# Modulation weights in ten tiles, paired low parts, scaling on GpSimd, half of group 0's rows on ScalarE

## The chip, the core and the metric

The kernel runs on one core of one Trainium2 chip. A core has five engines that take instructions each from a queue of its own: TensorE (PE, matrix products; its weight loads are shown apart as PEld), VectorE (DVE), ScalarE (ACT), GpSimd (POOL) and SyncE (SP), which here only issues DMA transfers. Engines wait for each other by semaphores; within one queue, order is kept. The metric is the device time of one execution in microseconds (us). A profile records one execution; "span" is the time from its first to its last instruction.

## The reference

One layer of a hybrid backbone. 2048 latent tokens `x` and 256 context tokens `ctx`, 1024 wide:

```
shift, scale, gate     = split(silu(c)     @ w_ada + b_ada)
shift_c, scale_c, ...  = split(silu(c_ctx) @ w_ada + b_ada)
h  = rmsnorm(x,   norm_w) * (1 + scale)   + shift
hc = rmsnorm(ctx, norm_w) * (1 + scale_c) + shift_c
p  = h  @ w_in                # 9216 columns: q, i, zf, zb, gate of 8 heads; 4 of the convolution
pc = hc @ w_in[:, :5120]
```

Then a gated linear recurrence in both directions over each head (its start state comes from the context), a gated three-tap convolution for the other half of the columns, `y = concat @ w_out`, `x + gate * y`, and a final RMS norm. All in float32.

## The kernel before

**Products.** To keep float32 precision with 16-bit matmuls, each operand is split into a high part (a cast to f16) and a low part (the difference, in f16 too); a product is three matmuls. The projection `h @ w_in` is done for a group of 512 tokens (`GW`; four groups) and two column blocks at a time by Winograd's form of Strassen's scheme (`seven`): seven products of half-size operands in place of eight. The token side of a group thus has seven operands, B11, T1, T2, B21, T3, B22, T4, each for four k (128 rows of the contraction). Group 0 starts differently: its first stretch ("plain" units) uses the four unsplit quarters B11, B12, B21, B22, and its T1 to T4 are made late (`late_turn`), in the fourth stretch.

**Start.** The order in the program is: load four x tiles of group 0 (128 tokens x 1024), their squares (L220), load and split the first pair of projection weights (`next_w(0)` at L1250: z gates of head 0), then `modulate` (L177). This multiplies the two conditioning vectors by the first 2048 columns of w_ada: for each of eight k two tiles of 128 x 1024 f32 are loaded (L182), four matmuls (L184) add to the PSUM tile `pada`, and `between(k)` transposes block k of group 0's scaled tokens and copies it out raw (L232, L239, L241). After k = 3 (`VQ_AT`) the second weight pair (V and Q of head 0) is loaded and split. The tiles of w_ada live in `f_tile` and `k_tile`, two of each: two k at a time. `modulate_end` and `affine` (L189, L198) turn `pada` into a scale and a shift per row. Then `turn` makes group 0's quarters: `rows(k)` scales and shifts the eight raw blocks in place (L246), `store` casts on ScalarE (L265) or GpSimd (L263), and subtracts on VectorE (L266).

**Weights.** `load_pair` (L327) loads two column blocks of w_in into "stage" tiles (three in all), sums absolute values on ScalarE (L341), finds a power-of-two scale (a one-column matmul, L139, and three small VectorE steps, L145 to L147), and splits them (L151 high on ScalarE, L152 low on VectorE) with four additions. A stage tile comes free with the last low part that reads it.

**Groups 1 to 3 and the context.** `norm_group` gives the steps: load, squares, a reciprocal root on VectorE (L125 to L131), scaling of each token tile by it (L225, VectorE), transposes (L232), rows (`rows`, L250 on ScalarE from PSUM), `combine` (the additions between quarters, L297 to L309) and `store`. Each operand of a k is a pair (high, low) of 256 columns, in a tile of tag "u" (eight of 1 KB a partition; the evacuations of `seven` use the same tag), and goes to DRAM (L268) by a DMA of SyncE. Once a group is complete, its seven operands are loaded back for all k (L1231) into the "hop" tiles (nine).

**Order.** The work is cut into 50 stretches; a stretch has units (products) and steps (norms, scan of a head, gates, weight splits), which are laid between the matmuls by weights (`PACE`). Stretch 0 holds the plain units and the context's units, and beside them the norms of the context and of group 1; stretches 1 and 2 hold the rest of group 2 and 3; stretch 3 group 0's late turns. Each engine then takes its instructions in an order fixed at build time: by the program's order, but something that is ready may pass something that isn't. A tile's slot is given again when all its readers are done, a store's landing included. The pools that matter: "ring" (ten slots of 2 KB: rows, combine's `t`, the scan's v, q, ks, kT, A, gates of the context, gate units), "u", "hop", "Q" (six), "stage".

Of the kernel before, what the change touches and what calls it, by code (L numbers as in the profile page):

```python
# [9 lines left out]
F32 = mybir.dt.float32  # L10
F16 = mybir.dt.float16
# [8 lines left out]
P = 128  # L20
# [40 lines left out]
def hybrid_layer(ctx: ExitStack, tc, x, cx, w_ada, b_ada, w_in, w_out, fnorm_w, small_d, masks, ident_d, sel_d, out):  # L61
# [29 lines left out]
    def pa_t(nm):  # L91
        return pa.tile([P, 512], F32, tag="pa", name=nm)
# [16 lines left out]
    def flat(t):  # L109
        return t.rearrange("p a b -> p (a b)")  # L110
# [63 lines left out]
        S.activation(sg2, cc, AF.Sigmoid)  # L174
        V.tensor_tensor(sc32[:, :, 0:2], cc, sg2, ALU.mult)

    def modulate(between):  # L177
        pada = pa_t("pada")
        for k in range(KT):
            wa = [(f_tile if j == 0 else k_tile)(f"wa{k}{j}") for j in range(2)]  # L180
            for j in range(2):
                SY.dma_start(flat(wa[j]), w_ada[0, k * P:(k + 1) * P, j * D:(j + 1) * D])  # L182
            for j in range(4):
                PE.matmul(pada[32 * j:32 * j + 32, :], sc32[:, k, :], wa[j // 2][:, j % 2],  # L184
                          start=k == 0, stop=k == KT - 1)
            between(k)
        return pada

# [19 lines left out]
    def norm_group(ntile, src, row0, m, nm, first_ops=None, space=q_tile):  # L208
        n = ntile * P
        xs = []  # L210
        ssq = sp.tile([P, 16], F32, tag="ssq", name=f"ssq_{nm}", bufs=4)

        def load(i):
            xt = space(f"xt_{nm}{i}")
            xt = flat(xt) if len(xt.shape) == 3 else xt
            SY.dma_start(xt, src[0, row0 + i * P: row0 + (i + 1) * P, :])
            xs.append(xt)

        def square(i):
            S.activation(junk, xs[i], AF.Square, accum_out=ssq[:, i:i + 1])  # L220

        def norm():
            rstd = rsqrt(ssq[:, :ntile], ntile, 1.0 / D, nm)
            for i in range(ntile):
                V.tensor_scalar(xs[i], xs[i], rstd[:, i:i + 1], None, ALU.mult)  # L225

        raws = {}

        def transposed(k):
            pt = pa_t(f"xT_{nm}{k}")  # L230
            for i in range(ntile):
                PE.transpose(pt[:, i * P:(i + 1) * P], xs[i][:, k * P:(k + 1) * P], ident)  # L232
            return pt

        def raw(k):
            pt = transposed(k)
            raws[k] = ring(f"h32_{nm}{k}")
            if k % 2:
                V.tensor_copy(raws[k], pt)  # L239
            else:  # L240
                S.activation(raws[k], pt, AF.Copy)  # L241

        def rows(k):
            if k in raws:
                h32 = raws[k]
                V.tensor_scalar(h32, h32, ab[:, m, 0, k:k + 1], ab[:, m, 1, k:k + 1], ALU.mult, ALU.add)  # L246
                return h32
            pt = transposed(k)
            h32 = ring(f"h32_{nm}{k}")
            S.activation(h32[:, :n], pt[:, :n], AF.Identity, bias=ab[:, m, 1, k:k + 1], scale=ab[:, m, 0, k:k + 1])  # L250
            return h32

        def store(op, k, src, cast, low=V):
            if m:
                i = ("B1", "B2", "D").index(op)
                hi, lo = hc[:, i, 0, k], hc[:, i, 1, k]
            elif first_ops is not None and op in first_ops:
                hi, lo = first_ops[op][:, 0, k], first_ops[op][:, 1, k]
            else:
                pair = hp.tile([P, 2, HW], F16, tag="u", name=f"hp{op}_{nm}{k}", bufs=8)  # L260
                hi, lo = pair[:, 0], pair[:, 1]
            if cast is G:
                G.tensor_scalar(hi, src, 1.0, 0.0, ALU.mult, ALU.add)  # L263
            else:
                S.activation(hi, src, AF.Copy)  # L265
            low.tensor_tensor(lo, src, hi, ALU.subtract)  # L266
            if m == 0 and (first_ops is None or op not in first_ops):
                SY.dma_start(Hd[row0 // GW][op][:, :, k], pair)  # L268
# [24 lines left out]
        def combine(k, a, b, whole):  # L293
            b11, b12, b21, b22 = a[:, :HW], a[:, HW:], b[:, :HW], b[:, HW:]
            t = ring(f"ht_{nm}{k}")
            t1, t2 = t[:, :HW], t[:, HW:]
            V.tensor_tensor(t1, b12, b11, ALU.subtract)  # L297
            if whole:
                store("B11", k, b11, S)
            store("T1", k, t1, G)  # L300
            V.tensor_tensor(t2, b22, t1, ALU.subtract)
            store("T2", k, t2, S)
            if whole:
                store("B21", k, b21, G)
            V.tensor_tensor(b12, b22, b12, ALU.subtract)
            store("T3", k, b12, S)
            if whole:
                store("B22", k, b22, G)
            V.tensor_tensor(b21, b21, t2, ALU.subtract)  # L309
            store("T4", k, b21, G)  # L310

        return ([paced("load", lambda i=i: load(i)) for i in range(ntile)],
                [paced("square", lambda i=i: square(i)) for i in range(ntile)] + [paced("norm", norm)],
                [paced("turn", lambda k=k: turn(k)) for k in range(HK)],
                [paced("late", lambda k=k: late_turn(k)) for k in range(HK)],
                [paced(0.0, lambda k=k: raw(k)) for k in range(KT)])
# [915 lines left out]
            hop.setdefault(wi_, {})[o] = t  # L1232
            taken[0] += 1

    x1_tiles = [hp.tile([P, D], F32, tag="hop", name=f"x1_{i}") for i in range(NCH)]
    x1_norm = norm_group(NCH, x, GW, 0, "x1", None, lambda nm: x1_tiles.pop(0))
    plain = {o: hop_tile(f"hop0{o}") for o in ("B11", "B12", "B21", "B22")}
    a21_ = hop_tile("a21")
    extra_a21 = [[a21_[:, hl, :, i * P:(i + 1) * P] for hl in range(2)] for i in range(2)]
# [9 lines left out]
    small_params()  # L1249
    next_w(0)  # L1250

    def between(k):
        first[4][k][1]()
        if k == VQ_AT:
            next_w(0)

    pada = modulate(between)
    ctx_norm = norm_group(2, cx, 0, 1, "c")
    for _, st in ctx_norm[0] + x1_norm[0]:
        st()  # L1260
# [263 lines left out]
```

## Time and profile before

| | |
|---|---|
| time, median of 3 | 2226.86 us (2222.09 to 2229.01) |
| profiled execution | 2224.16 us, span 2222.2 us |
| busy: PE, PEld | 2113.2 us (95%), 1466.6 us (66%) |
| busy: DVE, ACT, POOL | 1659.9 us (75%), 1158.3 us (52%), 112.5 us (5%) |
| mean granted TensorE clock | 0.988 |
| DMA | 309.89 MB, mean 139 GB/s |

How to read the lines below. A group's line has line, engine, operation, out<-in by the program's names, count, busy us, mean ns, and the idle time before it with what ended that. A source's line has min/median/max ns and first and last start. In a timeline: start, length, engine, line, operation, and in brackets the idle time of the engine before it and what it waited for. The chain of waits is followed back from the last instruction; "issue" is time in which nothing shown was waited for. SPq is SyncE's queue. The line numbers are those of the kernel before.

### The profile page before, as it was taken

To read this page: it belongs to the slowest core of one execution; us is meant where nothing else is said; L and a number is where in the kernel's file an instruction comes from. 1 tells how busy PE (TensorE), PEld (TensorE's weight loads), DVE (VectorE), ACT (ScalarE), POOL (GpSimd) and SP (SyncE) were. 2 spreads that over 40 slices of the span, in tenths; PEclk is the share of its full clock that TensorE was granted. 3 is DMA by queue.
4 is the path that set the end of the run, shared out by engine and by line. 5 is a ranking of instruction groups with operands and counts; after the bars stand their busy time and mean duration, and the time that the engine had idled before them with its cause. 6 is when DMAs were issued, how large, how long until landed. Compare 5 with 4: busy or idle time off the path is not lost.

```text
span 2222.2 us, 51962 instructions
## 1 busy us (share of the span) xinstructions
PE 2113.2 (95%) x21563; PEld 1466.6 (66%) x21563; DVE 1659.9 (75%) x3515; ACT 1158.3 (52%) x2313; POOL 112.5 (5%) x207
## 2 busy tenths in 40 slices
PE   4889899999999999999999999999999999999998
PEld 1767688888888888888888887444444444444443
DVE  6987877968779778788687786587678646677775
ACT  6655655665567555666676554354445313333332
POOL 0211100000000000000000000000000000000000
PEclk8889999999999999999999999999999999999999
DMA  8664343433243333333543357842343224633321
GB/s 324 223 212 169 103 137 103 153 95 117 82 158 112 106 120 119 108 111 122 191 134 131 126 183 248 240 137 101 108 138 116 68 90 157 232 106 122 120 99 57
DMA packets 191040, 309.89 MB, mean 139 GB/s; under 512 B 13138, under 2 KB 123090, under 8 KB 189012
## 3 DMA queue, kind: packets, MB, share of 16 engines
q1 hardware_dynamic: 188644, 302.64, 41.5%
q8 instruction: 169, 2.77, 0.5%
q10 hardware_dynamic: 2160, 3.93, 0.5%
q14 instruction: 67, 0.55, 0.1%
HBM read 241.50 MB, written 65.01 MB: 138 GB/s over the span
## 4 chain that ended last, share of the span: by engine, by line
PE 66%; DVE 15%; DMA 7%; ACT 6%; issue 4%; SPq 1%; POOL 1%; POOLq 0%; DVEq 0%; ACTq 0%
PE sa L839 8%; PE sa L841 7%; PE sa L840 7%; PE sb L839 4%; PE sb L840 3%; PE sb L841 3%; DMA ws_p<-in_w_in 3%; PE sa_o L839 2%; PE sa_o L841 2%; PE sa_o L840 2%; PE A L554 2%; PE T L602 2%; PE sc L839 2%; PE sc L841 2%; PE sc L840 2%
## 5 line engine op out<-in xcount | busy, mean ns | idle before, releaser
L840 PEld LDWEIGHTS <-e_p 128*128 128x128 f16 x1368 | 134.8, 99 | 66.8 <-issue 17.1
L414 DVE TENSOR_TENSOR K<-K,tot 128x512 f32<-128x512 f32 x192 | 132.0, 688 | 61.8 <-PE A L578 24.6
L839 PEld LDWEIGHTS <-e_p 128*128 128x128 f16 x1368 | 134.5, 98 | 60.2 <-issue 3.3
L841 PEld LDWEIGHTS <-e_p 128*128 128x128 f16 x1368 | 134.8, 99 | 53.1 <-issue 0.8
L421 DVE TENSOR_TENSOR Q<-Q,tot 128x512 f32<-128x512 f32 x192 | 132.6, 691 | 33.3 <-PE A L554 32.9
L537 ACT ACTIVATE km<-K 128x512 f32<-128x512 f32 x160 | 109.1, 686 | 86.3 <-DVE K L414 60.6
L840 PEld LDWEIGHTS <-whib_p 128*128 128x128 f16 x912 | 89.2, 98 | 45.5 <-issue 13.3
L586 POOL COPY A<-Ac 32x128 f32<-32x128 f32 x128 | 66.4, 519 | 1007.1 <-ACT A L582 649.2
L839 PEld LDWEIGHTS <-whib_p 128*128 128x128 f16 x912 | 89.1, 98 | 40.8 <-issue 3.7
L840 PEld LDWEIGHTS <-whia_p 128*128 128x128 f16 x912 | 89.3, 98 | 37.9 <-issue 6.3
L839 PEld LDWEIGHTS <-whia_p 128*128 128x128 f16 x912 | 89.2, 98 | 37.5 <-issue 0.8
L841 PEld LDWEIGHTS <-wloa_p 128*128 128x128 f16 x912 | 89.3, 98 | 34.3
L841 PEld LDWEIGHTS <-wlob_p 128*128 128x128 f16 x912 | 89.2, 98 | 34.3
L151 ACT ACTIVATE e_p<-ws_p,sc_p 128x512 f16<-128x512 f32 x108 | 77.2, 716 | 61.4 <-DVE ws_p L376 39.4
L341 ACT ACTIVATE junk<-ws_p 128x1024 f16<-128x1024 f32 x72 | 76.0, 1055 | 55.7 <-DMA ws_p<-in_w_in 55.2
L846 ACT ACTIVATE u<-sa,sx_w 128x256 f32<-128x256 f32 (+1 forms) x114 | 59.8, 524 | 70.9 <-PE sa L841 56.1
L554 PE MATMUL A<-Q,km 128*32 128x32 f32 x5120 | 77.9, 202 | 12.4 <-DVE Q L421 6.4
L554 PEld LDWEIGHTS A<-Q,km 128*32 128x32 f32 x5120 | 58.9, 112 | 46.4 <-issue 20.3
L762 ACT ACTIVATE cv<-c,small 128x512 f32<-128x512 f32 (+1 forms) x36 | 24.2, 671 | 109.2 <-DVE c L780 48.9
L152 DVE SCALAR_TENSOR_TENSOR e_p<-ws_p,sc_p,e_p 128x512 f16<-128x512 f32 x108 | 78.0, 743 | 2.5 <-ACT e_p L151 2.4
L846 ACT ACTIVATE p<-sb,sx_w 128x256 f32<-128x256 f32 (+1 forms) x114 | 59.3, 520 | 35.6 <-PE sb L841 34.0
L846 ACT ACTIVATE p<-sa,sx_w 128x256 f32<-128x256 f32 (+1 forms) x114 | 58.8, 516 | 32.2 <-PE sa L841 32.1
(865 smaller groups left out, 6881.7 us busy)
## 6 DMA issues: line engine op xcount, KB each, us to landing
ws_p<-in_w_in SPq DMA_DIRECT2D x72, 512.0 KB, 4.4
y_o<-yT SPq DMA_DIRECT2D x32, 512.0 KB, 3.8
wa<-in_w_ada SPq DMA_DIRECT2D x16, 512.0 KB, 5.4
Gd<-zs SPq DMA_DIRECT2D x32, 256.0 KB, 3.5
sg<-Gd SPq DMA_DIRECT2D x32, 256.0 KB, 4.1
yT<-y SPq DMA_DIRECT2D x32, 256.0 KB, 2.3
wos_a<-in_w_out SPq DMA_DIRECT2D x16, 512.0 KB, 4.6
yT<-sg SPq DMA_DIRECT2D x64, 128.0 KB, 2.6
```

The source lines that it names most:

```text
L151: S.activation(hi, src, AF.Copy, scale=st[:, 0:1])
L152: V.scalar_tensor_tensor(lo, src, st[:, 0:1], hi, ALU.mult, ALU.subtract)
L341: S.activation(junk.rearrange("p (k n) -> p k n", k=KT), stage[i], AF.Abs, accum_out=r)
L414: V.tensor_tensor(m, m, sub(cur, nb + 1, [[2, np_], [-(nb + 1), 2], [0, B]]), ALU.mult)
L421: V.tensor_tensor(m, m, sub(cur, 1, [[2, np_], [nb - 1, 2], [0, B]]), ALU.mult)
L537: S.activation(sub(s.km, 0, [[2 * B, n // (2 * B)], [B, 2], [1, B]]), mix(s.K, n, B, n // (2 * B)), AF.Copy)
L554: PE.matmul(pt[j * SB:(j + 1) * SB, ch * SB:(ch + 1) * SB], s.km[:, o:o + SB], mix(s.qf, n, B, SB // (2 * B), o), start=True, stop=True)
L586: G.tensor_copy(A3[js, :, js], s.Ac[js])
L839: PE.matmul(ps, hi[:, k], rh, start=start and k == 0, stop=False, skip_group_check=not start)
L840: PE.matmul(ps, hi[:, k], right(name, 1, k), start=False, stop=False, skip_group_check=not start)
L841: PE.matmul(ps, lo[:, k], rh, start=False, stop=k == nk - 1, skip_group_check=not start)
L846: S.activation(r, ps, AF.Copy, scale=sx)
```

## The change

- **Ten tiles.** `modulate` loads w_ada into ten tiles: two f, two K, two Q and four hop tiles, so five k at a time. The loads of the first five k are issued ahead of all of its matmuls; a further k is loaded when the matmuls of the k five before it are in the program. The V/Q weight pair is loaded (and split) after the load of k = 3, ahead of the modulation's matmuls and of the raw transposes, where it stood after `between(3)`. The hop tiles of group 1's tokens are taken when they are loaded, behind the modulation, and no longer ahead of everything.
- **Scaling on GpSimd.** The scaling of token tiles goes to GpSimd for the context and groups 1 to 3; group 0's stays on VectorE.
- **Half of group 0's rows on ScalarE.** Of the eight raw blocks, the four with k >= HK are scaled and shifted by ScalarE.
- **Rows of two operands.** In `combine`, T1 and T2 lie side by side in one tile, B11 and T3 in another, B21 and B22 in the third. For groups 1 to 3 these are cast and subtracted 512 columns at a time (`store2`), T4 alone with 256; for group 0's late turns T1 with T2, T3 and T4 alone. The (high, low) pairs come from "ring" in place of "u". The DMAs to DRAM stay one for each operand.

```diff
+    def wa_hop(nm):
+        return hp.tile([P, D], F32, tag="hop", name=nm)
+
-    def modulate(between):
+    def modulate(between, vq):
         pada = pa_t("pada")
+        homes = [f_tile, k_tile, f_tile, k_tile, q_tile, q_tile] + [wa_hop] * 4
+
+        def load(k):
+            wa[k] = []
+            for j in range(2):
+                t = homes[(2 * k + j) % len(homes)](f"wa{k}{j}")
+                t = t if len(t.shape) == 3 else t.rearrange("p (a b) -> p a b", a=2)
+                SY.dma_start(flat(t), w_ada[0, k * P:(k + 1) * P, j * D:(j + 1) * D])
+                wa[k].append(t)
+
+        wa = {}
+        room = len(homes) // 2
+        for k in range(room):
+            load(k)
+            if k == VQ_AT:
+                vq()
         for k in range(KT):
-            wa = [(f_tile if j == 0 else k_tile)(f"wa{k}{j}") for j in range(2)]
-            for j in range(2):
-                SY.dma_start(flat(wa[j]), w_ada[0, k * P:(k + 1) * P, j * D:(j + 1) * D])
             for j in range(4):
-                PE.matmul(pada[32 * j:32 * j + 32, :], sc32[:, k, :], wa[j // 2][:, j % 2],
+                PE.matmul(pada[32 * j:32 * j + 32, :], sc32[:, k, :], wa[k][j // 2][:, j % 2],
                           start=k == 0, stop=k == KT - 1)
+            if k + room < KT:
+                load(k + room)
             between(k)
...
             for i in range(ntile):
-                V.tensor_scalar(xs[i], xs[i], rstd[:, i:i + 1], None, ALU.mult)
+                if first_ops is None:
+                    G.tensor_scalar(xs[i], xs[i], rstd[:, i:i + 1], None, ALU.mult)
+                else:
+                    V.tensor_scalar(xs[i], xs[i], rstd[:, i:i + 1], None, ALU.mult)
...
                 h32 = raws[k]
-                V.tensor_scalar(h32, h32, ab[:, m, 0, k:k + 1], ab[:, m, 1, k:k + 1], ALU.mult, ALU.add)
+                if k < HK:
+                    V.tensor_scalar(h32, h32, ab[:, m, 0, k:k + 1], ab[:, m, 1, k:k + 1], ALU.mult, ALU.add)
+                else:
+                    S.activation(h32, h32, AF.Identity, bias=ab[:, m, 1, k:k + 1], scale=ab[:, m, 0, k:k + 1])
...
-                pair = hp.tile([P, 2, HW], F16, tag="u", name=f"hp{op}_{nm}{k}", bufs=8)
...
+        def store2(ops, k, row, eng):
+
+            n2 = len(ops)
+            pair = rp.tile([P, 2, n2, HW], F16, tag="ring", name=f"hp{ops[0]}_{nm}{k}")
+            hi, lo = [pair[:, i].rearrange("p a b -> p (a b)") for i in range(2)]
+            cast(eng, hi, row)
+            V.tensor_tensor(lo, row, hi, ALU.subtract)
+            for i, op in enumerate(ops):
+                SY.dma_start(Hd[row0 // GW][op][:, :, k], pair[:, :, i])
...
             V.tensor_tensor(t1, b12, b11, ALU.subtract)
+            V.tensor_tensor(t2, b22, t1, ALU.subtract)
+            store2(("T1", "T2"), k, t, S)
+            V.tensor_tensor(b12, b22, b12, ALU.subtract)
             if whole:
-                store("B11", k, b11, S)
-            store("T1", k, t1, G)
-            V.tensor_tensor(t2, b22, t1, ALU.subtract)
-            store("T2", k, t2, S)
-            if whole:
-                store("B21", k, b21, G)
-            V.tensor_tensor(b12, b22, b12, ALU.subtract)
-            store("T3", k, b12, S)
-            if whole:
-                store("B22", k, b22, G)
+                store2(("B11", "T3"), k, a, S)
+                store2(("B21", "B22"), k, b, G)
+            else:
+                store2(("T3",), k, b12, S)
             V.tensor_tensor(b21, b21, t2, ALU.subtract)
-            store("T4", k, b21, G)
+            store2(("T4",), k, b21, G)
...
-    x1_tiles = [hp.tile([P, D], F32, tag="hop", name=f"x1_{i}") for i in range(NCH)]
-    x1_norm = norm_group(NCH, x, GW, 0, "x1", None, lambda nm: x1_tiles.pop(0))
+    x1_norm = norm_group(NCH, x, GW, 0, "x1", None, wa_hop)
...
-    def between(k):
-        first[4][k][1]()
-        if k == VQ_AT:
-            next_w(0)
-
-    pada = modulate(between)
+    pada = modulate(lambda k: first[4][k][1](), lambda: next_w(0))
```

(`cast` is the old choice between GpSimd and ScalarE as a function of its own; `store` keeps the context's operands and group 0's plain quarters.)

More of the change, by code (lines that the diff above doesn't have):

```diff
@@ L251, in rows, with cast, store @@
             return h32
-        def store(op, k, src, cast, low=V):
+        def cast(eng, hi, src):
+            if eng is G:
+                G.tensor_scalar(hi, src, 1.0, 0.0, ALU.mult, ALU.add)
+            else:
+                S.activation(hi, src, AF.Copy)
+        def store(op, k, src, eng):
             if m:
@@ L256, in store @@
                 hi, lo = hc[:, i, 0, k], hc[:, i, 1, k]
-            elif first_ops is not None and op in first_ops:
+            else:
                 hi, lo = first_ops[op][:, 0, k], first_ops[op][:, 1, k]
-            else:
-                pair = hp.tile([P, 2, HW], F16, tag="u", name=f"hp{op}_{nm}{k}", bufs=8)
[L261 to L268, printed above, removed]
+            cast(eng, hi, src)
+            V.tensor_tensor(lo, src, hi, ALU.subtract)
+        def store2(ops, k, row, eng):
[6 more added lines that the diff above has]
+                SY.dma_start(Hd[row0 // GW][op][:, :, k], pair[:, :, i])
         def turn(k):
@@ L297, in combine @@
             V.tensor_tensor(t1, b12, b11, ALU.subtract)
+            V.tensor_tensor(t2, b22, t1, ALU.subtract)
+            store2(("T1", "T2"), k, t, S)
+            V.tensor_tensor(b12, b22, b12, ALU.subtract)
             if whole:
-                store("B11", k, b11, S)
-            store("T1", k, t1, G)
-            V.tensor_tensor(t2, b22, t1, ALU.subtract)
-            store("T2", k, t2, S)
-            if whole:
-                store("B21", k, b21, G)
-            V.tensor_tensor(b12, b22, b12, ALU.subtract)
-            store("T3", k, b12, S)
-            if whole:
-                store("B22", k, b22, G)
+                store2(("B11", "T3"), k, a, S)
+                store2(("B21", "B22"), k, b, G)
+            else:
+                store2(("T3",), k, b12, S)
             V.tensor_tensor(b21, b21, t2, ALU.subtract)
-            store("T4", k, b21, G)
+            store2(("T4",), k, b21, G)
         return ([paced("load", lambda i=i: load(i)) for i in range(ntile)],
```

## The prediction

> **What bounds the kernel now.** I read the busy time by stage first, because an average over 2222 us hides the opening. Columns: stretch, length, busy time of PE, weight load, VectorE (DVE), ScalarE (ACT) and GpSimd (POOL), granted clock, DMA share, GB/s.
>
> ```profile
> span 2222.2 us, 51962 instructions
> ```
>
> ```profile
> 14.00:44.50 30.50, 22.00 (x98) 6.43 (x98) 21.00 (x36) 14.96 (x23) 0.00 (x0) 0.96 0.90 320
> ...
> 48.40:58.50 10.10, 5.68 (x25) 3.54 (x25) 10.10 (x27) 6.67 (x14) 4.47 (x8) 0.50 0.84 272
> 58.50:74.30 15.80, 15.80 (x141) 13.81 (x139) 14.35 (x53) 11.55 (x24) 4.15 (x8) 0.97 0.66 268
> 74.30:100.00 25.70, 18.47 (x152) 15.57 (x149) 22.19 (x64) 19.20 (x39) 9.26 (x16) 0.93 0.61 175
> 100.00:160.00 60.00, 48.08 (x572) 37.48 (x573) 54.60 (x136) 36.90 (x76) 12.05 (x23) 0.83 0.73 226
> ...
> 260.00:1389.00 1129.00, 1107.60 (x15685) 955.17 (x15683) 872.88 (x1961) 688.81 (x1543) 60.42 (x116) 1.00 0.40 132
> ```
>
> After 260 us TensorE is busy 1107.6 of 1129 us: what comes earlier to that point ends earlier. Every edit acts before it. From 48.4 to 58.5 us VectorE is busy all the time (10.10 of 10.10) and TensorE about half; from 100 to 160 us VectorE is at 54.6 of 60. There a microsecond of VectorE can be a microsecond of the end. The chain of waits says what ends last before 58 us:
>
> ```profile
> 24.39 0.33 SPq L333
> ...
> 24.81 4.71 DMA wa<-in_w_ada
> ...
> 35.31 7.22 DMA wa<-in_w_ada
> ...
> 42.57 1.94 PE pada L184 x4
> ...
> 44.53 0.70 DVE ada_r L191
> ...
> 48.48 4.06 DVE h_x L246 x8
> ```
>
> The modulation's weights are last; then 3.95 us of small steps (44.53 to 48.48); then VectorE's eight row operations and the low parts.
>
> **Ten tiles.** Ahead of the last weight tile go 24 transfers of 512 KB (4 of x, 4 of projection weights, 16 of modulation weights), 12.6 MB. DMA in the first 48 us, in 40 slices of 1.2 us, with the issues:
>
> ```profile
> GB/s 0 76 208 389 399 410 411 419 423 427 406 420 393 85 177 396 348 215 410 416 222 195 382 399 413 423 355 119 321 198 338 321 307 270 413 406 423 430 403 365
> ...
> wa<-in_w_ada SPq DMA_DIRECT2D x16, 512.0 KB, 5.4
> xt_x<-in_x SPq DMA_DIRECT2D x4, 512.0 KB, 5.0
> ws_p<-in_w_in SPq DMA_DIRECT2D x4, 512.0 KB, 5.9
> ```
>
> Where enough is asked for, it moves about 415 GB/s; the holes (85, 215, 195, 119, 198) are times in which the queue waited for tiles. Without holes 12.6 MB from 2 us on land by 32.4; four matmuls (1.94) make 34.3 against 44.5: pada can end 10.2 us earlier at most. The HBM limit per core of about 358 GB/s that the Trainium skill gives (DMA: Bandwidth & Descriptors, Specifications) speaks against so much: by it the same bytes would take 35.2 us, and the bound would be 5.4; the slices above it (423, 430) say otherwise here.
>
> But one wait of the queue isn't removed. SyncE's queue:
>
> ```profile
> 4.79 15.23 SPq L182 DMA_DIRECT2D wa<-in_w_ada  x8
> 20.07 4.65 SPq L333 DMA_DIRECT2D ws_p<-in_w_in  x2
> 24.81 10.87 SPq L182 DMA_DIRECT2D wa<-in_w_ada  x8
> ```
>
> The second tile of the V/Q weights went out at 24.39, as "stage" has three tiles and the first pair holds two until its low parts are done. That stays, and the queue held to the program's order: the last eight loads stood behind it. With it now behind k=3's load, 15 transfers (7.9 MB) are ahead of it and done by 21; from 24.4 on, 9 remain (4.7 MB, 11.4 us) after some 2.3 us to the first bytes (an estimate: the 5.4 us to landing is spent in a full queue). The last tile lands near 38.1, TensorE ends near 40.0: **−4.5**, the value I take.
>
> The V/Q load is itself a step that moves: two issues, two absolute-sum passes, eight ScalarE casts, eight low parts, four additions and a one-column matmul now stand before all eight raw transposes in the program. VectorE's order tells the price:
>
> ```profile
> 39.00 0.68 DVE L239 COPY h_x<-xT_x 128x512 f32<-128x512 f32 x1
> 44.53 0.69 DVE L191 COPY ada_r<-pada 128x512 f32<-128x512 f32 x1 [4.85 <-PE pada L184]
> ```
>
> Today its low parts end at 39.0, one raw copy follows, and 4.85 us are idle. If all four of VectorE's raw copies (0.68 each) fall behind, VectorE is free at 41.7, 1.7 us past the 40.0 at which I let pada end; the copies have VectorE's wait for the second V/Q tile (from 24.4 until it lands) to run in, so I price this at nothing; without that cover it takes 1.7 of the 4.5. And where the low parts still end at 39.0, no earlier pada helps past 39.0 + 3.95 = 42.95 for the first row, 5.5 before 48.48. The other end: if TensorE kept the V/Q scale matmul (30.55 below) ahead of all modulation matmuls, k=0's tiles would come free only near 31.6, six transfers (7.6 us plus 2.3) and four matmuls would follow, and pada would end at 43.5, −1.0. Against it: that matmul runs amid the modulation's today.
>
> ```profile
> 30.55 0.18 PE L139 MATMUL ss_p<-rb_p 128*128 128x1 bf16 x1
> ```
>
> Bounds −5.5 to −1.0.
>
> **Half of group 0's rows on ScalarE.** VectorE from 48 to 62 us, and two rows of the page:
>
> ```profile
> L266 DVE TENSOR_TENSOR hop0B<-h_x,hop0B 128x256 f16<-128x256 f32 x16 | 6.0, 447 | 0.0
> L246 DVE TENSOR_SCALAR h_x<-h_x,ab 128x512 f32<-128x512 f32 x8 | 4.1, 587 | 0.0
> ```
>
> ```profile
> L414 DVE TENSOR_TENSOR K<-K,tot 128x512 f32<-128x512 f32 x192 | 132.0, 688 | 61.8 <-PE A L578 24.6
> ...
> L537 ACT ACTIVATE km<-K 128x512 f32<-128x512 f32 x160 | 109.1, 686 | 86.3 <-DVE K L414 60.6
> ```
>
> The eight take 4.06 us of the chain; four fewer is **−2.0**. ScalarE gains 4 × 0.686 = 2.7 beside 6.67 in a stretch of 10.1, so it can just carry them; if squares of x1 come ahead of them in its order, nothing is won: bounds −2.0 to 0.
>
> **Token scaling on GpSimd.** Six tiles at 61 to 67 us (context and group 1), four each for groups 2 and 3:
>
> ```profile
> L225 DVE TENSOR_SCALAR xt_x<-xt_x,rsy_x x12: 747/748/753, 14.0 to 154.6; 128x1024 f32<-128x1024 f32 x12
> L225 DVE TENSOR_SCALAR x<-x,rsy_x x4: 745/822/897, 62.4 to 66.6; 128x1024 f32<-128x1024 f32 x4
> L225 DVE TENSOR_SCALAR xt_c<-xt_c,rsy_c x2: 745/748/752, 60.9 to 61.6; 128x1024 f32<-128x1024 f32 x2
> ...
> L263 POOL TENSOR_SCALAR hpT_x<-h_x x12: 405/754/1318, 79.1 to 202.0; 128x256 f16<-128x256 f32 x12
> ```
>
> ```profile
> PE xT_x L232 <- DVE xt_x L225: 5.3, 2, 4.9
> ```
>
> VectorE loses 14 instructions, about 10.8 us of busy time. GpSimd's price at 1024 elements isn't shown: no less than the 0.405 of 256, no more than four times 1.318 (5.3). I take four times the fastest, 1.6, as the operation is the same with four times the elements. The Trainium skill (GPSIMD Engine Reference, section 3.1) gives 1.03 cycles an element at 1.2 GHz where the ports bind, by which I estimate 0.9 us and group 1 scaled 4 us earlier than by 1.6; no row here shows it. Context and x1 then take 6 × 1.6 = 9.6 us after their root, against 6.6 (60.9 to 67.5) in which VectorE did them among other work: 3 us later, hidden while TensorE has plain units (15.80 of 15.80 to 74.3); if they ran out, it would cost 3. Group 2's scaling is waited for (4.9 us): on GpSimd 6.4 against 3.0, 3.4 later, while its root comes earlier, as VectorE stretched it over its other work. Behind the scaling on GpSimd's queue wait the casts of the same groups and the diagonal copies of the scan. I take **−1** for all, bounds −6 (two groups' scaling off a busy VectorE) to +4 (group 2's delay and a little of group 1's).
>
> **Low parts of two operands.** Per k of groups 1 to 3, seven low parts become three wide and one narrow:
>
> ```profile
> L266 DVE TENSOR_TENSOR hpB_x<-h_x,hpB_x x36: 399/415/617, 75.8 to 201.2; 128x256 f16<-128x256 f32 x36
> ```
>
> 7 × 0.415 = 2.9 against 3 × 0.688 + 0.415 = 2.5: 0.43 a k, 5.1 over twelve. ScalarE: three narrow casts become two wide, GpSimd: four become one wide and one narrow, little either way. The stores, seven a k, stay as many on SyncE's queue. Between 74 and 160 us, where VectorE is short, eight k's give 3.4 at best; I take **−1.5**, bounds −3.4 to 0.
>
> The same edit moves the pairs' homes: from eight "u" slots of their own to the ten "ring" slots that the rows, the scan and the gates share. What it removes and what it meets:
>
> ```profile
> 84.94 0.41 POOL L263 TENSOR_SCALAR hpT_x<-h_x 128x256 f16<-128x256 f32 x1 [2.44 <-DMA Hd1B<-hpB_x]
> ...
> 88.00 0.41 POOL L263 TENSOR_SCALAR hpT_x<-ht_x 128x256 f16<-128x256 f32 x1 [2.65 <-DMA Hd1B<-hpB_x]
> ```
>
> ```profile
> 110.86 0.78 ACT L250 ACTIVATE h_x<-xT_x,ab 128x512 f32<-128x512 f32 x1 [1.00 <-DVE h_x L309]
> ```
>
> ```profile
> DMA to landing us min/median/max: 2.1/2.4/5.8
> ```
>
> (The last row is the operand stores'.) GpSimd waits 5.1 us for a "u" slot to land, which goes; ScalarE waits for the last reader of the k before, which I read as a full ring. Between: **0**, bounds −5 to +20 (rival a).
>
> **Sum.** −4.5 − 2.0 − 1 − 1.5 + 0 = −9. The profiled execution took 2224.16 us around its span of 2222.2; less 9 it is 2215. It lies 2.7 under the median of three, 2226.86, so for a median I say 2218.
>
> **Rivals.** (a) *The ring starves (slower).* While the scan holds v, vT, q, A and two kT, and a k its two rows and t, nine of ten slots are taken. A pair lives about 0.7 + 0.7 + 2 × 0.6 + 2.4 = 5 us (cast and low part of 512 by the rows above, two issues, landing). Through one slot four pairs take 20 us; today the last k of group 3 takes 9.8 from its first row (195.30) to its last store's issue (205.05), and the next stretch's operands are fetched at once:
>
> ```profile
> 195.30 1.45 ACT L250 ACTIVATE h_x<-xT_x,ab 128x512 f32<-128x512 f32 x2 [5.19 <-PE xT_x L232]
> ```
>
> ```profile
> 204.41 0.55 SPq L1231 DMA_DIRECT2D hop3B<-Hd3B  x1
> 205.05 0.51 SPq L268 DMA_DIRECT2D Hd3T<-hpT_x  x1
> ```
>
> So such a k delays the next stretch by 10.2 us, two of them by 20.4: 2218 + 20.4 = 2238. It decides from where fewer than two slots are left, as two make 10 us a k, today's pace. For it: the full ring, and that casts wait in order on ScalarE with the evacuations behind them. Against: pairs are half as many, and "u" is left to the evacuations. (b) *The lead isn't kept*: scaling comes late (+4), the ring costs 2, and opening and rows give 6.5: −0.5, 2226 (2222 to 2230). For it: from 74 to 160 us TensorE already stands 19 of 86 us, and what it waits for there is group 1's and 2's chain, which now runs over GpSimd. Against: that chain starts earlier by what the opening gives. (c) *No hole in the loads*: the last loads pass the waiting tile, rows start when VectorE is free of V/Q (−5.5), and VectorE's relief counts nearly in full: −5.5 − 2 − 4 − 3 = −14.5, 2212. For it: the stretches in which VectorE is busy all the time; against: the queue's order today.
>
> **Chances.** Forecast 0.43 (2214 to 2222), (c) 0.15, (b) 0.24, (a) 0.18. About 0.3% (6.7 us) is what these runs can tell from no change: faster is below 2220.2, slower above 2233.5. The forecast's case gives 0.36 of its 0.43 to faster and the rest to the same, (c) all to faster, (b) all to the same; (a) gives 0.15 to slower and 0.03 to the same: faster 0.51, same 0.34, slower 0.15. The likeliest's own range is 2214 to 2222; with (c) and most of (a) 2207 to 2237.
>
> **What would show it.** Right: the last modulation load issued before 36 us, pada's end near 40, first row operation near 44, VectorE's rows and low parts in 8 us, TensorE busy throughout from about 52; SyncE still waiting for the low parts of the first pair near 24. Scaling on GpSimd near 1.6 us. Wrong: modulation matmuls all after 30 us; scaling over 2.5 us with transposes waiting for it; rows, casts or evacuations waiting for stores of pairs between 100 and 210 us, and hop loads of stretches 2 and 3 later than now.

## The result and the profile after

The changed kernel takes 2252.71 us (median of 4 runs, 2250.36 to 2252.85) against 2226.86 (2222.09 to 2229.01): 1.0113 times the time before, with a 95% interval of 1.0099 to 1.0126. It is slower by 26 us, where 2218 and a range of 2207 to 2237 were forecast. The profiled execution took 2252.69 us with a span of 2250.9.

The busy time by stretch, for the windows that the prediction read (columns as there):

```profile
48.40:58.50 10.10, 8.02 (x37) 4.92 (x36) 9.49 (x35) 7.20 (x15) 3.84 (x6) 0.50 0.75 246
58.50:74.30 15.80, 12.24 (x101) 9.94 (x99) 6.21 (x18) 10.63 (x22) 14.73 (x9) 0.98 0.74 301
74.30:100.00 25.70, 18.82 (x128) 15.45 (x128) 15.95 (x42) 11.99 (x20) 15.40 (x12) 0.80 0.19 57
100.00:160.00 60.00, 38.83 (x477) 30.28 (x476) 49.63 (x104) 38.69 (x72) 11.73 (x15) 0.87 0.65 203
260.00:1389.00 1129.00, 1105.73 (x15727) 955.70 (x15725) 878.27 (x1969) 695.64 (x1556) 64.15 (x122) 1.00 0.40 132
```

From 58.5 to 74.3 us GpSimd, the fifth column of busy times, is busy for 14.73 of 15.80 us (before: 4.15), VectorE for 6.21 (before: 14.35), and TensorE no longer all the time. From 100 to 160 TensorE works 38.83 us where it worked 48.08. After 260 it is as full as before: the loss is made before that. What GpSimd does is shown first by the scaling's line, then by the waits of TensorE between 44 and 290 us:

```profile
L244 POOL TENSOR_SCALAR xt_x<-xt_x,rsy_x x12: 2837/2842/3261, 64.3 to 179.3; 128x1024 f32<-128x1024 f32 x12
L244 POOL TENSOR_SCALAR xt_c<-xt_c,rsy_c x2: 2843/2844/2844, 57.2 to 60.0; 128x1024 f32<-128x1024 f32 x2
```

```profile
PE xT_x L253 <- POOL xt_x L244: 15.0, 8, 3.1
...
PE sa L868 <- DMA hop1B<-Hd1B: 2.7, 1, 2.7
```

A tile takes 2.84 us, where VectorE took 0.75 and the prediction 1.6, and the transposes wait for it. The timeline of GpSimd shows that the tiles run one behind the other, with the context's casts (hc) between them:

```profile
64.30 3.11 POOL L244 TENSOR_SCALAR xt_x<-xt_x,rsy_x 128x1024 f32<-128x1024 f32 x1
67.39 0.40 POOL L279 TENSOR_SCALAR hc<-h_c 128x256 f16<-128x256 f32 x1
67.76 5.93 POOL L244 TENSOR_SCALAR xt_x<-xt_x,rsy_x 128x1024 f32<-128x1024 f32 x2
73.67 0.40 POOL L279 TENSOR_SCALAR hc<-h_c 128x256 f16<-128x256 f32 x1
74.05 2.84 POOL L244 TENSOR_SCALAR xt_x<-xt_x,rsy_x 128x1024 f32<-128x1024 f32 x1
...
100.27 2.84 POOL L244 TENSOR_SCALAR xt_x<-xt_x,rsy_x 128x1024 f32<-128x1024 f32 x1
...
170.82 11.30 POOL L244 TENSOR_SCALAR xt_x<-xt_x,rsy_x 128x1024 f32<-128x1024 f32 x4 [10.49 <-DVE rsy_x L131]
```

Group 1 is scaled by 76.89 us, group 2 by 103.11, group 3 by 182.12. The loads of group 3's operands then come at 230.5 to 233.9 us, 26 later than before. Before:

```profile
L1231 SPq DMA_DIRECT2D hop3B<-Hd3B x3: 383/434/548, 204.4 to 207.8; - x3
```

After:

```profile
L1260 SPq DMA_DIRECT2D hop3B<-Hd3B x3: 382/435/547, 230.5 to 233.9; - x3
```

### The profile page after: what moved, and what is told of

The parts are those of the page before. It is cut to its first block, busy times and chain, and to the rows that moved or that the text cites. A ratio compares the mean times of both kernels' runs of the same rounds, so it can differ in the third digit from the quotient of the medians.

```text
span 2250.9 us, 51820 instructions
## 1 busy us (share of the span) xinstructions
PE 2122.6 (94%) x21563; PEld 1472.6 (65%) x21563; DVE 1652.3 (73%) x3457; ACT 1163.4 (52%) x2305; POOL 137.9 (6%) x193
## 4 chain that ended last, share of the span: by engine, by line
PE 64%; DVE 13%; DMA 5%; ACT 5%; issue 3%; SPq 1%; POOL 0%; POOLq 0%; ACTq 0%; DVEq 0%
PE sa L868 8%; PE sa L870 7%; PE sa L869 7%; PE sb L868 3%; PE sb L869 3%; PE sb L870 3%; DMA ws_p<-in_w_in 2%; PE T L631 2%; PE sa_o L868 2%; PE sa_o L869 2%; PE sa_o L870 2%; PE A L583 2%; PE sc L868 2%; PE sc L870 2%; PE sc L869 2%
## 5 line engine op out<-in xcount | busy, mean ns | idle before, releaser
L151 ACT ACTIVATE e_p<-ws_p,sc_p 128x512 f16<-128x512 f32 x108 | 77.3, 716 | 59.2 <-DVE ws_p L405 37.4
L583 PE MATMUL A<-Q,km 128*32 128x32 f32 x5120 | 77.9, 202 | 5.7 <-DVE Q L450 3.7
```

The lines of the kernel that those rows point to most:

```text
L151: S.activation(hi, src, AF.Copy, scale=st[:, 0:1])
L583: PE.matmul(pt[j * SB:(j + 1) * SB, ch * SB:(ch + 1) * SB], s.km[:, o:o + SB], mix(s.qf, n, B, SB // (2 * B), o), start=True, stop=True)
```

## The experiments

Each kernel is compared with runs of the kernel before on the same chip, whose median lay between 2226.70 and 2228.96 us; the ratio is to these, with its 95% interval. "Theory S" is that scaling on GpSimd makes the loss; its rivals are that the pairs crowd the ring (R) and that the new order of the opening costs what its loads gain (O).

### One part undone, one part alone

**Scaling back on VectorE**, all else as changed:

```diff
-                    G.tensor_scalar(xs[i], xs[i], rstd[:, i:i + 1], None, ALU.mult)
+                    V.tensor_scalar(xs[i], xs[i], rstd[:, i:i + 1], None, ALU.mult)
```

> The changed kernel with token scaling back on VectorE, all else as changed. Theory S (scaling): GpSimd takes 2.84 us for a 128x1024 tile, one after the other in its queue, and that holds up the transposes of groups 1, 2 and 3; the rest of the change gains. Then 2215 to 2224 us, the first stores of group 1 before 76 us, the operands of the second stretch loaded before 115 us. Theory R (ring): the pairs crowd the ring; then the time stays at 2245 or more and rows or casts wait for stores. If both share the loss, some 2235.

2226.36 us, 0.9997 (0.9988 to 1.0005). The whole loss is gone, and no gain is left in its place. Theory S holds for the loss; its expectation that the other parts gain 3 us or more does not, and group 1's first stores went out at 77.9, not before 76. In this trace the last of group 3's loads (hop3B) starts at 208.3 us, where it started at 207.8 before the change: whatever the opening gained is gone by then.

**The scaling alone**, in the kernel before (the same line, VectorE to GpSimd):

> The kernel before with nothing but the scaling of the context and groups 1 to 3 on GpSimd. Theory S: the whole loss and no gain of the other parts to set against it: 2250 to 2260 us, scaling at 2.8 us a tile, group 1's first store near 90 us. Theory R: at most 2232.

2254.53 us, 1.0125 (1.0109 to 1.0140). The scaling alone makes the loss, and group 1's first store goes out at 89.3.

**The rows of two operands alone** (the new `combine`, `cast` and `store2`, pairs in the ring):

> The kernel before with nothing but the rows of two operands, pairs in ring slots. Theory S: the pairs are a small gain or none, 2222 to 2228 us. Theory R: 2245 us or more, the last stores of groups 2 and 3 later than 141 and 206 us.

2227.39 us, 1.0001 (0.9993 to 1.0010). No difference, and the ring theory falls: groups 2 and 3 store last at 141.2 and 203.5 us (before: 140.0 and 205.1). In the trace with scaling back on VectorE the longest wait for a pair's store between 60 and 210 us is 3.1 us, as long as in the kernel before.

**Ten tiles alone** (the new `modulate`, V/Q moved, group 1's tiles taken later):

> The kernel before with nothing but the ten tiles (with the V/Q pair moved ahead of the modulation's matmuls). Theory S, and the changed kernel's trace in which the modulation's sum was read out 2.1 us earlier: 2.1 us off the opening and up to that off the end, 2223 to 2226 us. Rival O (order): the V/Q work ahead of the raw blocks and the group 1 tiles that are taken later cost as much as the loads gain: 2227 us or more.

2225.66 us, 0.9999 (0.9990 to 1.0008). No difference that can be measured. Rival O doesn't explain that: in the trace the last of group 3's loads starts 3.7 us earlier than before (204.1 against 207.8).

**Ten tiles and half rows**, scaling and pairs as before:

> The kernel before with the ten tiles and half of group 0's rows on ScalarE; scaling on VectorE and pairs in their own slots as before. By the prediction's terms (4.5 and 2.0 less) 2221 us. Theory L (the lead is lost late): up to the reload for the convolution (1340 us) this kernel is 5 to 6 us ahead of the kernel before, and of this at most 2 us are left at the end, as TensorE then waits longer in one piece (over 3 us near 1420 us) and gets a lower clock: 2224 to 2227 us.

2225.12 us, 0.9993 (0.9984 to 1.0002). The lead in its trace is 3.6 us at group 3's loads and 3.1 near 1356, not 5 to 6; the time is where theory L put it, but the interval reaches over 1.

### Which group, and what the tile's price is

**Groups 2 and 3 alone on GpSimd**, then **the context and group 1 alone**, both with all other parts of the change:

```diff
-                if first_ops is None:
+                if nm in ("x2", "x3"):      # the other kernel: ("c", "x1")
                     G.tensor_scalar(xs[i], xs[i], rstd[:, i:i + 1], None, ALU.mult)
```

> The changed kernel with the scaling of the context and group 1 back on VectorE; groups 2 and 3 stay on GpSimd. Theory S with the delay laid where the changed kernel's stores stood back (group 1: 19 us of 26): 2231 to 2236 us. Rival Q (each group's scaling costs its own 8 us, whatever goes before): 2240 to 2245 us.

> The changed kernel with the scaling of groups 2 and 3 back on VectorE; the context and group 1 stay on GpSimd. Theory S as above: 2242 to 2248 us, as group 1's delay of 19 us goes through to the end. Rival Q: 2233 to 2238 us. If group 1's delay were hidden by later waits: under 2231 us.

2243.06 us, 1.0074 (1.0059 to 1.0090), and 2235.46 us, 1.0041 (1.0027 to 1.0055). Rival Q is right in both. I had read the 19 us by which group 1's stores were late as group 1's own cost; its last stores stood behind group 2's scaling on GpSimd. Against the kernel with scaling on VectorE (0.9997) groups 2 and 3 cost 0.77% or 17.1 us, the context and group 1 0.44% or 9.8. Eight tiles of 2.84 - 0.75 = 2.09 us are 16.7, four are 8.4: within the intervals, of 3 to 4 us either way, each of the twelve tiles of the three groups costs its full extra price.

**The price by itself**: operations on GpSimd alone at the start of the kernel before.

```diff
+    for n_ in (256, 512, 1024):
+        G.tensor_scalar(xa[:, :n_], xa[:, :n_], 1.0, 0.0, ALU.mult, ALU.add)
+    for n_ in (256, 512, 1024):
+        G.tensor_scalar(xa[:, :n_], xa[:, :n_], nw0, None, ALU.mult)
...
+    G.tensor_tensor(xa, xa, xa, ALU.mult)
```

> The kernel before with twelve operations on GpSimd at the start, in order at 256, 512 and 1024 elements each: f16 from f32 by two constants; f32 from f32 by two constants; f32 from f32 by one number per partition; f16 from f32 by one number per partition; then an f32 product of two tiles, and a scaling of 128x1024 on ScalarE. Its time is of no interest. The prediction took the operation for the cast with four times the elements (1.6 us at 1024). If the number per partition makes the price, the first two forms take 0.4, 0.8 and 1.6 us and the other two 0.7, 1.4 and 2.8 us; if the f32 output makes it, the second and third form take 2.8 us at 1024 and the first and fourth 1.6.

The groups of GpSimd's instructions up to 40 us (count | busy us, mean ns | idle before):

```profile
L1258 POOL TENSOR_SCALAR mh<-mx,small 128x1024 f16<-128x1024 f32 x1 | 3.2, 3157 | 0.1
L1256 POOL TENSOR_SCALAR mx<-mx,small 128x1024 f32<-128x1024 f32 x1 | 2.8, 2844 | 0.1
...
L1259 POOL TENSOR_TENSOR mx<-mx 128x1024 f32<-128x1024 f32 x1 | 1.9, 1893 | 0.1
...
L1254 POOL TENSOR_SCALAR mx<-mx 128x1024 f32<-128x1024 f32 x1 | 1.1, 1059 | 0.1
L1252 POOL TENSOR_SCALAR mh<-mx 128x1024 f16<-128x1024 f32 x1 | 1.0, 1047 | 0.1
L1256 POOL TENSOR_SCALAR mx<-mx,small 128x256 f32<-128x256 f32 x1 | 0.9, 926 | 0.1
...
L1254 POOL TENSOR_SCALAR mx<-mx 128x256 f32<-128x256 f32 x1 | 0.4, 408 | 0.1
```

The number per partition (operand `small`) makes the price: 2844 ns where two constants take 1059, with f16 output 3157 against 1047, and already at 256 elements 926 against 408. Constants are cheaper, too, than four times the cast of 256 (1.6 us), by which the prediction and this expectation went: 1.06. The product of two whole tiles is cheaper (1893) than the product with one number per partition. ScalarE scaled the same tile in 1.15 us.

### Only the size, or the step too

Three kernels with all other parts of the change put the scaling at other prices: as a product with the root spread over the columns, by constants with one column by the root (this one leaves out the normalization of the other columns), and on ScalarE.

```diff
-                    G.tensor_scalar(xs[i], xs[i], rstd[:, i:i + 1], None, ALU.mult)
+                    G.tensor_tensor(xs[i], xs[i], sub(rstd, i, [[0, D]]), ALU.mult)      # first
+                    G.tensor_scalar(xs[i][:, 0:1], xs[i][:, 0:1], rstd[:, i:i + 1], None, ALU.mult)   # second
+                    G.tensor_scalar(xs[i], xs[i], 1.0, 0.0, ALU.mult, ALU.add)
+                    S.activation(xs[i], xs[i], AF.Copy, scale=rstd[:, i:i + 1])      # third
```

> The changed kernel with its scaling on GpSimd done as a product of two tiles, the root spread over the 1024 columns: 1.9 us a tile for 2.84. Theory P (price): the loss goes with the price above VectorE's 0.75, 26.3 us for 2.09 us, so 14 us for 1.14: 2238 to 2243 us. Theory H (hidden up to a point, as the prediction had it near 1.6 us): 2225 to 2231 us. Theory B (the queue is the loss, whatever the price): 2246 us or more.

> The same with one column of a tile scaled by the root and the whole tile then multiplied by constants, so that the work still waits for the root but the normalization of the other columns is left out: some 1.25 us a tile in two instructions on GpSimd. Theory P: 26.3 / 2.09 x 0.5 = 6 us over the kernel with scaling on VectorE, 2230 to 2235 us. Theory H: 2222 to 2227 us. Theory B: 2240 us or more.

> The same with the scaling on ScalarE, 1.15 us a tile: VectorE has it off its hands as with GpSimd, and no cast on GpSimd stands behind it. Theory P (price alone, on any queue): 5 us more than on VectorE, 2229 to 2233 us. If GpSimd's queue made the loss: 2223 to 2227 us. If VectorE's relief is worth what the prediction gave it: 2222 us or less.

| scaling | us a tile (median) | group 1, 2, 3 scaled by (us) | time | ratio (95%) | over VectorE |
|---|---|---|---|---|---|
| VectorE | 0.75 | 70.3, 88.1, 156.6 | 2226.36 | 0.9997 (0.9988 to 1.0005) | |
| GpSimd, constants | 1.33 | 70.0, 91.1, 165.6 | 2234.32 | 1.0027 (1.0014 to 1.0039) | 6.7 |
| GpSimd, product | 1.97 | 72.9, 96.3, 172.5 | 2239.99 | 1.0060 (1.0034 to 1.0085) | 14.0 |
| GpSimd, number per partition | 2.84 | 76.9, 103.1, 182.1 | 2252.71 | 1.0113 (1.0099 to 1.0126) | 25.8 |
| ScalarE | 1.14 | 74.4, 92.5, 157.0 | 2224.60 | 0.9990 (0.9979 to 1.0001) | -1.6 |

The last column is the difference of the ratios by 2227 us. On GpSimd twelve tiles times the price over 0.75 are 7.0, 14.6 and 25.1 us: theory P, and no price hides in the total. Group by group it isn't so even: by constants group 1 is scaled no later than by VectorE, group 2 by 3.0 us and group 3 by 9.0. On ScalarE theory P fails: 4 us late at the scaling of groups 1 and 2, the kernel loads group 1's first operand earlier than with VectorE (104.0 against 106.2 us) and is level at group 3's scaling. The extra slices of 0.4 us, 4.8 in all, are made good there and not on GpSimd. What makes them good isn't shown; VectorE, which has less to do, is a candidate.

The ScalarE kernel once more in more rounds, with single pairs in their own slots, and alone in the kernel before:

> The changed kernel with its scaling on ScalarE, in more rounds. If VectorE's relief is real: 2222 to 2225 us, with the interval below 1. If it was noise: 2225 to 2229, the interval over 1.

> Ten tiles, half rows, scaling on ScalarE, single pairs in their own slots. If relief and opening add: 2220 to 2224 us. If there is no relief to be had: as without the move, 2225.

> The kernel before with nothing but the scaling on ScalarE. Relief real: 2 us less than before, 2224 to 2226 us. Price alone (0.4 us a tile more, four tiles in each of three groups): 5 us more, 2231 to 2233 us. Neither: 2226 to 2229.

2227.53 us, 1.0005 (0.9996 to 1.0014); 2225.52, 0.9994 (0.9985 to 1.0003); 2226.83, 1.0004 (0.9994 to 1.0015). (Of the second, one execution of eleven took 10.6 ms; it is left aside.) The 2224.60 lay in the noise: moved to ScalarE, the scaling wins nothing and costs nothing that these runs can tell.

### Why nothing else gains

Two ideas: that VectorE's scaling isn't on the path at all, and that the opening's lead is lost near 1420 us, where TensorE waits for an evacuation that stands on ScalarE behind the absolute sums of a weight still under way.

```diff
-                PE.transpose(pt[:, i * P:(i + 1) * P], xs[i][:, k * P:(k + 1) * P], ident)
+                PE.matmul(pt[:, i * P:(i + 1) * P], xs[i][:, k * P:(k + 1) * P], dg[0][:, i], start=True, stop=True)
```

> Ten tiles, half rows, and no scaling of token tiles at all for the context and groups 1 to 3: the transposing product takes a diagonal of the reciprocal roots (one operation of 512 elements on VectorE for a group) in place of the identity. If VectorE's 10.8 us of scaling were on the path, as the prediction's gain for GpSimd had it, its removal gives up to 2 us a group: 2219 to 2223 us, with 6 us of lead at 1340. If the lead is lost near 1420 us whatever its size: 2223 to 2226.

```diff
-                    next_w(wk[2], 4)
+                    next_w(wk[2], 12 if kind == "pair" else 4)
```

> The kernel before, with the splitting of a new weight pair begun twelve steps after its load is issued instead of four, in the last stretches (pairs of groups) alone, so that ScalarE need not stand at the absolute sums for a load that is still under way (8 us near 1420 us), with evacuations behind it. Theory L: TensorE's wait near 1420 us (2.9 us in the profile of before) shrinks and the time falls by 1 to 3 us: 2224 to 2226. If the wait is not on the path: 2227.

> The same later splitting, with the ten tiles and half of group 0's rows on ScalarE. Theory L: the opening's lead of some 3 us now reaches the end: 3 us less than the kernel before with later splitting alone, 2220 to 2223 us. If the lead is lost for another cause: within 1 us of it.

> Ten tiles, half rows, the diagonal in place of the scaling, and the later splitting in the last stretches. Theory L: all leads reach the end: 2214 to 2220 us. If they don't: 2223 or more.

Diagonal in place of the scaling: 2225.97 us, 0.9994 (0.9985 to 1.0003), as ten tiles and half rows without it (0.9993). In its trace VectorE's busy time falls from 1659.7 to 1653.5 us, but TensorE's from 44 to 260 us grows from 174.8 to 184.5, as a product with a diagonal is recorded as two matmuls where a transpose is one (192 for 96 in groups 1 to 3). So this run doesn't tell what VectorE's relief is worth, and in the runs with ScalarE relief and price come together. Later splitting alone: 2231.52, 1.0021 (1.0012 to 1.0031); with ten tiles and half rows 2228.76, 1.0014 (1.0004 to 1.0023); with the diagonal too 2230.45, 1.0015 (1.0005 to 1.0025). It made the kernel slower. The waits of TensorE from 1340 to 2200 us with later splitting:

```profile
PE sc L839 <- DVE c L784: 8.5, 5, 2.0
PE sa L839 <- ACT p L846: 5.9, 4, 3.2
```

and in the kernel before:

```profile
PE sa L839 <- ACT p L846: 4.1, 4, 2.9
PE sc L839 <- DVE c L784: 2.7, 4, 0.8
```

The wait that was to shrink (ACT p) grew, and one for VectorE came on top: theory L is neither shown nor refuted, as the edit didn't shrink the wait. Whether the opening's lead would reach the end without the gap near 1420 us is open: the two kernels with later splitting differ by 2.8 us in favour of the one with the lead, but their intervals overlap.

## Why the prediction was wrong

**Ten tiles (-4.5).** The loads did what was said, and the end of the sum came where it was forecast. SyncE's queue, TensorE and VectorE of the changed kernel:

```profile
13.02 11.66 SPq L362 DMA_DIRECT2D ws_p<-in_w_in  x2
24.73 3.87 SPq L189 DMA_DIRECT2D wa<-in_w_ada  x8
```

```profile
29.34 1.92 PE L200 MATMUL pada<-wa,sc 128*32 128x512 f32 x2 [6.42 <-DMA wa<-in_w_ada]
...
38.70 1.05 PE L200 MATMUL pada<-wa,sc 128*32 128x512 f32 x4 [0.24 <-DMA wa<-in_w_ada]
39.69 2.10 PE L253 MATMUL xT_x<-ident,xt_x 128*128 128x128 f32 x12
```

```profile
28.05 0.69 DVE L385 TENSOR_TENSOR s_p<-ws_p 128x512 f32<-128x512 f32 x1 [3.11 <-DMA ws_p<-in_w_in]
...
39.66 1.41 DVE L260 COPY h_x<-xT_x 128x512 f32<-128x512 f32 x2
41.82 0.69 DVE L260 COPY h_x<-xT_x 128x512 f32<-128x512 f32 x1 [0.75 <-PE xT_x L253]
42.43 0.68 DVE L209 COPY ada_r<-pada 128x512 f32<-128x512 f32 x1
```

The queue waits for the first pair's low parts and issues the second V/Q tile by 24.7 (forecast 24.4), the last load is issued at 28.6, the sum ends at 39.75 (forecast 40.0). It is read out at 42.43 only: three raw copies stand between. The prediction named this price, 1.7 us, and set it to nothing, as the copies were to run while VectorE waited for V/Q. VectorE did wait for V/Q (3.11 us before 28.05), but there was little to copy: TensorE, whose matmuls and transposes alternate, stood 6.42 us at a modulation weight that was loaded behind V/Q, and made 12 of the 32 transposes only after the sum. With the wait for the last of them (0.75) the copies took 2.7. So 2.1 of the 4.5 came (1.2 in the run of ten tiles alone), and the first row began at 45.81, not 43.95.

**Half rows (-2.0).** With ten tiles alone the last of group 0's low parts began at 57.0 us, with half rows too at 55.7: 1.3 came there. At group 3's loads both kernels have the same lead (204.1 and 204.2 against 207.8): in these two traces nothing of it went further.

**Scaling on GpSimd (-1): the step that failed.** It measured +26, first because of the price, then because the price isn't hidden. The 1.6 us were four times a cast of 256 by two constants; the scaling takes a number per partition, another kind of operand, and 2.84. By the prediction's own arithmetic 2.84 would have made 8.4 us for group 2 alone, but it took over only the small price into its range: the row gave up to 5.3 us a tile, and the upper end of +4 was worked out from 1.6. And at 1.6 us there would have been a loss all the same, an estimate of some 10 us (12 x 0.85, between the 6.7 and 14.0 measured at 1.33 and 1.97). The prediction hid the price behind plain units and set VectorE's relief against it; at none of the three prices on GpSimd does a gain show. With the scaling on ScalarE, at little more than VectorE's price, the time is the same (1.0005 and 1.0004): the relief is worth nothing there, or no more than the 4.8 us of price that it may have paid. "A microsecond of VectorE can be a microsecond of the end" was read from busy shares (10.10 in 10.10, 54.6 in 60); an engine can be that busy with work that nobody waits for, and no run here gained from less of it. What is on the path with GpSimd is the delay from a group's root to its last scaled tile: the four transposes of a row block need all four tiles, TensorE waits 15.0 us for them, and the next group's root and scaling come behind. The Trainium skill (GPSIMD Engine Reference, section 3.1), by which the prediction estimated 0.9 us, is near the price by constants (1.06), not that by a number per partition.

**Low parts of two operands (-1.5).** VectorE saves more than was said. Low parts between 70 and 205 us with pairs (scaling on VectorE):

```profile
L295 DVE TENSOR_TENSOR hpB_x<-h_x,hpB_x 128x512 f16<-128x512 f32 x24 | 15.5, 682 | 0.9 <-POOL hpB_x L276 0.7 <-ACT hpB_x L278 0.2
L295 DVE TENSOR_TENSOR hpT_x<-ht_x,hpT_x 128x512 f16<-128x512 f32 x12 | 8.2, 686 | 0.8 <-ACT hpT_x L278 0.4
...
L295 DVE TENSOR_TENSOR hpT_x<-h_x,hpT_x 128x256 f16<-128x256 f32 x12 | 5.2, 430 | 3.9 <-POOL hpT_x L276 3.9
```

and before:

```profile
L266 DVE TENSOR_TENSOR hpB_x<-h_x,hpB_x 128x256 f16<-128x256 f32 x36 | 16.6, 461 | 0.0
L266 DVE TENSOR_TENSOR hpT_x<-ht_x,hpT_x 128x256 f16<-128x256 f32 x24 | 11.9, 504 | 2.6 <-POOL hpT_x L263 2.3 <-ACT hpT_x L265 0.2
L266 DVE TENSOR_TENSOR hpT_x<-h_x,hpT_x 128x256 f16<-128x256 f32 x24 | 10.3, 431 | 3.2 <-POOL hpT_x L263 3.1
```

38.8 us become 28.9, a saving of 9.9, twice the 5.1 of the prediction. No gain is measured all the same (1.0001). With pairs alone group 1's B stores run from 77.3 to 102.4 us, where they ran from 76.4 to 98.7; yet the last of group 3's loads starts at 206.2, 1.6 us earlier than before, and that of stretch 35 at 1355.0, 4.4 earlier. So that trace, too, has a lead that the median doesn't show.

**Pair homes (0) and the rivals.** The runs have the homes only together with the low parts; the two together measured nothing, and rival (a), the starving ring, didn't come. Rival (b) pointed at the right chain, groups 1 and 2 over GpSimd, with a price of 4 us in place of 26. Rival (c) fell: the queue kept its hole. The case that came stood only in the prediction's list of what would show it wrong: scaling over 2.5 us with transposes waiting.

**The lead that stays unseen.** With ten tiles alone, and with half rows too, the opening gives 3 to 4 us, and they are there 1100 us later. With the pairs added (scaling on VectorE) they aren't: the last of group 3's loads starts at 208.3 us, 0.5 later than before, though either part alone is ahead there. The gains don't add up; what takes the lead away before 208 us is open. Loads for the reload of stretch 35, kernel before and ten tiles alone:

```profile
L1231 SPq DMA_DIRECT2D hop35B<-Hd3B x3: 319/319/432, 1338.0 to 1359.4; - x3
```

```profile
L1249 SPq DMA_DIRECT2D hop35B<-Hd3B x3: 320/320/430, 1333.8 to 1354.8; - x3
```

Then TensorE's wait and the stretch from 1420 to 1440 us, first before, then ten tiles alone:

```profile
1429.11 0.38 PE L839 MATMUL sa<-C1T,e_p 128*128 128x512 f16 x1 [2.86 <-ACT p L846]
```

```profile
1420.00:1440.00 20.00, 17.14 (x80) 7.73 (x79) 9.28 (x15) 6.55 (x11) 0.00 (x0) 1.00 0.58 217
```

```profile
1427.02 0.58 PE L857 MATMUL sa<-C1T,e_p 128*128 128x512 f16 x1 [4.61 <-ACT p L864]
```

```profile
1420.00:1440.00 20.00, 15.39 (x62) 6.34 (x60) 7.78 (x13) 6.54 (x11) 0.00 (x0) 0.83 0.42 150
```

TensorE's wait there is 2.9 us in one piece before and 4.6 with ten tiles, and the mean clock granted over these 20 us is 0.83 in place of 1.00: a matmul of 512 columns takes 0.58 to 0.63 us for the 4.6 us after the wait, 0.38 ahead of it. Waits of 3.2 us (later splitting), 3.4 (half rows too) and 3.8 (pairs alone) there went with 0.91, 0.83 and 0.91. That fits the Trainium skill (TensorE: Matmul & The Clock Gate, part 1), by which an idle window of some 3.4 us lowers the clock. The longer wait (1.7 us) and the eleven slower matmuls after it (one every 0.42 us for 0.22, some 2.2 us) take some 4 of the 4.6 us of lead in these two executions. As the cause of the medians it is argued, not shown.

## What to carry to other kernels

Price an operation by a row with the same kinds of operands, not only the same name and size: on GpSimd a number per partition took 2.7 times what constants took. A high busy share doesn't say that an engine's work is waited for: here fourteen scalings of 0.75 us went from VectorE to ScalarE without a gain in the time, while on GpSimd each microsecond more on the short chain from a root to its transposes came out at the end, to within the noise. When a bound from the rows is wide (0.405 to 5.3 us), carry both ends through the sum into the range.

## What the runs showed of the hardware

GpSimd's price goes with the operand: 2.84 us for 128x1024 with a number per partition, 1.89 for a product of two tiles, 1.06 by constants. And a short VectorE step that began soon after the start of a GpSimd scaling could be stretched. VectorE in the changed kernel, beside the context's two tiles (GpSimd, from 57.18 and 60.0 us):

```profile
57.21 0.17 DVE L125 TENSOR_SCALAR rsv_x<-ssq_x 128x4 f32<-128x4 f32 x1 [0.19 <-ACT junk L238]
57.41 0.90 DVE L126 TENSOR_SCALAR rsa_x<-rsv_x 128x4 int32<-128x4 int32 x1
...
59.57 0.16 DVE L131 SCALAR_TENSOR_TENSOR rsy_x<-rsa_x,rsy_x 128x4 f32<-128x4 f32 x1
60.16 0.97 DVE L131 SCALAR_TENSOR_TENSOR rsy_x<-rsa_x,rsy_x 128x4 f32<-128x4 f32 x1
```

The steps that began 0.23 us after the first tile's start and some 0.15 after the second's took 0.8 us longer; the one that began 0.03 after the first's didn't, and steps in the middle of a tile kept their 0.16 us. The Trainium skill (SBUF — State Buffer, Who interferes with whom) has VectorE instructions with two SBUF inputs contend with GpSimd's reads. The last row, a step with two inputs, agrees that the two meet, but shows 0.8 us of it near the start alone and not over the tile's 2.84; and the step at 57.41, stretched as well, has one input. How much of the loss such steps make, beside the tiles' own price, isn't separated by these runs.
